# Instance norm on one core: 32 units of 4 MB become four of 4 MB and fourteen of 8 MB with 64 KB rows

## The chip, the cores and the metric

The kernel runs on one core of a Trainium2 chip. The metric is device time in microseconds (us) of one execution, as the median of several. The core has a matrix engine (PE), a vector engine (DVE), a scalar engine (ACT), a general engine (POOL), a sequencer for transfers (SP), and 16 DMA engines that move data between the device memory and the on-chip memory. SP and ACT each have a hardware DMA queue of their own (q1 is that of SP, q10 that of ACT); both queues feed the same 16 DMA engines.

## The reference

Each of 4 x 8 x 16 = 512 channels of 256 x 256 float32 is normalised by its own mean and variance, and scaled by a gamma that is shared over the batch. Input and output are 134.2 MB each.

```python
x: (4, 8, 16, 256, 256) float32, gamma: (8, 16) float32
mu = x.mean(axis=(3, 4), keepdims=True)
var = ((x - mu) ** 2).mean(axis=(3, 4), keepdims=True)
x_norm = (x - mu) / np.sqrt(var + 1e-5)
out = x_norm * gamma[None, :, :, None, None]
```

## The kernel before

The input is one flat array, cut into U = 32 units of 128 rows (one row per partition) by F = 8192 elements. A row is 32 KB, a unit is 4 MB, and a channel takes S = 8 rows, so that a unit holds K = 16 channels. A unit lives in one of AHEAD = 6 slots (`xt`) of on-chip memory.

The work of one unit, in the loop from line 104 on:

- DVE sums each row (`reduce_sum`, line 106) while ACT squares the same row and accumulates the squares (line 107; the squares themselves go to `junk`). Both results go to `st`.
- PE multiplies `st` with `navg`, a matrix that holds -1/65536 where two rows belong to the same channel (line 115). The result `ps` has minus the mean and minus the mean square of a row's channel, in every row.
- A short chain over one column follows: `nvar` on DVE (116), `std` on ACT (120), `rstd` and `scale` on DVE (124, 126).
- DVE normalises the unit in place (line 135). In unit 0 alone ACT does three eighths of it (line 132), and needs a `shift` for that (line 131).
- ACT's queue stores the unit (line 139). Then SP's queue loads the unit that is to use the same slot (lines 141 and 48), once that store has landed.

The order within each engine is the order of the program: nothing reorders it. The first six loads are issued before everything else, units 1 and 3 on ACT's queue and the others on SP's. All stores are on ACT's queue. Before the loop POOL fills `navg`, and PE spreads gamma over the rows of `g_col` from `g_rep`, a copy with each gamma repeated (lines 80 to 91). A `touch` of 16 x 128 zeros is written to the output early by POOL (lines 52 to 54): 512 bytes at the start of every eighth row of unit 0, which the store of unit 0 writes over later.

Of the kernel before, what the change touches and what calls it, by code (L numbers as in the profile page):

```python
# [1 line left out]

# [4 lines left out]

F32 = mybir.dt.float32
U8 = mybir.dt.uint8
ALU = mybir.AluOpType  # L10
ACTF = mybir.ActivationFunctionType
AX = mybir.AxisListType


@with_exitstack
def kernel(
    ctx: ExitStack,
    tc: tile.TileContext,
    x: bass.AP,
    gamma: bass.AP,  # L20
    out: bass.AP,
):
    nc = tc.nc
    B, G, C, H, W = x.shape
    P = nc.NUM_PARTITIONS
    HW = H * W
    n_ch = B * G * C
    S = 8
    K = P // S
    F = HW // S  # L30
    U = n_ch // K
    NG = (G * C) // K
    AHEAD = 6
    assert HW % S == 0 and (G * C) % K == 0

    xv = x.rearrange("b g c h w -> (b g c h w)").rearrange("(u p f) -> u p f", p=P, f=F)
    ov = out.rearrange("b g c h w -> (b g c h w)").rearrange("(u p f) -> u p f", p=P, f=F)
    gv = gamma.rearrange("g c -> (g c)")

    data = ctx.enter_context(tc.tile_pool(name="data", bufs=1))  # L40
    singles = ctx.enter_context(tc.tile_pool(name="singles", bufs=1))
    psum = ctx.enter_context(tc.tile_pool(name="psum", bufs=4, space=bass.MemoryType.PSUM))
    ctx.enter_context(tc.manual_schedule())

    slots = [data.tile([P, F], F32, name=f"xt{i}") for i in range(AHEAD)]

    def load(u, queue):
        queue.dma_start(out=slots[u % AHEAD][:], in_=xv[u])  # L48


    g_row = singles.tile([1, G * C], F32, name="g_row")
    touch = singles.tile([16, 128], F32, name="touch")
    nc.vector.memset(touch[:], 0.0)  # L53
    nc.gpsimd.dma_start(out=ov[0][0::S, 0:128], in_=touch[:])  # L54
    nc.gpsimd.dma_start(out=g_row[:], in_=gv[None, :])  # L55
    for u in range(AHEAD):
        load(u, nc.scalar if u in (1, 3) else nc.sync)

    eps_t = singles.tile([P, 1], F32, name="eps_t")
    nc.gpsimd.memset(eps_t[:], 1e-5)  # L60
    one = singles.tile([1, 1], F32, name="one")
    nc.gpsimd.memset(one[:], 1.0)
    navg = singles.tile([P, K, S], F32, name="navg")
    nc.gpsimd.memset(navg[:], -1.0 / HW)  # L64
    nc.gpsimd.affine_select(  # L65
        out=navg[:], in_=navg[:], pattern=[[-S, K], [0, S]], compare_op=ALU.is_ge,
        fill=0.0, base=0, channel_multiplier=1,
    )
    nc.gpsimd.affine_select(  # L69
        out=navg[:], in_=navg[:], pattern=[[S, K], [0, S]], compare_op=ALU.is_ge,  # L70
        fill=0.0, base=S - 1, channel_multiplier=-1,
    )
    navg_w = navg[:].rearrange("p k s -> p (k s)")
    root_eps = singles.tile([P, 1], F32, name="root_eps")
    nc.scalar.activation(out=root_eps[:], in_=eps_t[:], func=ACTF.Sqrt)  # L75
    g_rep = singles.tile([1, NG, K, S], F32, name="g_rep")
    g_ps = psum.tile([P, NG], F32, name="g_ps", bufs=1)
    g_col = singles.tile([P, NG], F32, name="g_col")

    nc.vector.tensor_copy(  # L80
        out=g_rep[:],
        in_=g_row[:].rearrange("o (n k) -> o n k", n=NG).unsqueeze(3).to_broadcast([1, NG, K, S]),
    )
    for n in range(NG):
        nc.tensor.matmul(  # L85
            out=g_ps[:, n : n + 1],
            lhsT=g_rep[:, n].rearrange("o k s -> o (k s)"),
            rhs=one[:],
            start=True, stop=True,
        )  # L90
    nc.vector.tensor_copy(out=g_col[:], in_=g_ps[:])  # L91

    junk = singles.tile([P, F], U8, name="junk")

    st = singles.tile([P, U, 2], F32, name="st")
    nvar = singles.tile([P, U], F32, name="nvar")
    std = singles.tile([P, U], F32, name="std")
    rstd = singles.tile([P, U], F32, name="rstd")
    scale = singles.tile([P, U], F32, name="scale")

    shift = singles.tile([P, 1], F32, name="shift")

    squares = []
    for u in range(U):
        t = slots[u % AHEAD]
        nc.vector.reduce_sum(out=st[:, u, 0:1], in_=t[:], axis=AX.X)  # L106
        square = nc.scalar.activation(  # L107
            out=junk[:], in_=t[:], func=ACTF.Square, accum_out=st[:, u, 1:2],
        )
        if u:  # L110

            tc.declare_no_dep(square.ins, squares[-1].ins, reason="junk, ordered by the root between")
        squares.append(square)
        ps = psum.tile([P, 2], F32, name="ps")
        nc.tensor.matmul(out=ps[:], lhsT=navg_w, rhs=st[:, u], start=True, stop=True)  # L115
        nc.vector.tensor_scalar(  # L116
            out=nvar[:, u : u + 1], in0=ps[:, 0:1], scalar1=ps[:, 0:1],
            scalar2=ps[:, 1:2], op0=ALU.mult, op1=ALU.add,
        )
        nc.scalar.activation(  # L120
            out=std[:, u : u + 1], in_=nvar[:, u : u + 1], func=ACTF.Sqrt,
            bias=eps_t[:], scale=-1.0,
        )
        nc.vector.reciprocal(out=rstd[:, u : u + 1], in_=std[:, u : u + 1])  # L124
        g = u % NG
        nc.vector.tensor_mul(  # L126
            out=scale[:, u : u + 1], in0=rstd[:, u : u + 1], in1=g_col[:, g : g + 1],
        )
        cut = F * 5 // 8 if u == 0 else F
        if cut < F:  # L130
            nc.vector.tensor_mul(out=shift[:], in0=ps[:, 0:1], in1=scale[:, u : u + 1])  # L131
            nc.scalar.activation(  # L132
                out=t[:, cut:], in_=t[:, cut:], func=ACTF.Identity, bias=shift[:], scale=scale[:, u : u + 1],
            )
        nc.vector.tensor_scalar(  # L135
            out=t[:, :cut], in0=t[:, :cut], scalar1=ps[:, 0:1], scalar2=scale[:, u : u + 1],
            op0=ALU.add, op1=ALU.mult,
        )
        nc.scalar.dma_start(out=ov[u], in_=t[:])
        if u + AHEAD < U:  # L140
            load(u + AHEAD, nc.sync)


# [1 line left out]
_INS = ['x', 'gamma']  # L145
_OUTS = [((4, 8, 16, 256, 256), 'float32')]


# [23 lines left out]
```

## Time and profile before

| What | Value |
|---|---|
| Time, median of 3 runs | 626.87 us (626.64 to 627.07) |
| Span of the profiled execution, first to last instruction | 625.2 us |
| Profiled execution outside its span, taken as median less span | 1.7 us |
| DVE busy | 441.8 us (71%) |
| ACT busy | 241.8 us (39%) |
| PE busy | 21.4 us (3%) |
| Moved by the DMA engines | 268.46 MB, mean 429 GB/s |
| Load of a unit (SP's queue), issue to landing, median | 38.5 us |
| Store of a unit (ACT's queue), issue to landing, median | 62.5 us |

The profile page gives busy times, the span in 40 slices with the share of the time in which the DMA engines were busy, the DMA queues with their share of the 16 engines' time, and the costliest groups of instructions with what they waited for. "Share of 16 engines" means that 100% would be all 16 engines busy from the first to the last instruction. The trace also has a record of each single DMA packet (queue, size, start and duration); where a packet's duration is told in the text, it is from these records. In this kernel each row of 32 KB is one packet.

### The profile page before, as it was taken

The numbers are of one execution on the slowest core, as the hardware profiler recorded it, in microseconds if no ns is written. First come the engines' busy times: TensorE is split into PE (matmuls) and PEld (weight loads), VectorE is DVE, ScalarE is ACT, GpSimd is POOL, SyncE is SP. The second block draws the span as 40 slices with busy tenths as digits, with TensorE's granted clock in tenths as the row PEclk, the third lists the DMA queues.
The fourth block names the chain that finished last, engine by engine and source line by source line (L and its number), as shares of the span: only waits on it lengthen the run. The fifth ranks groups of instructions, "written<-read, shape, count | busy, mean of one in ns | idle before, by whom it ended". The sixth has DMA issues, their size and how long they took to land.

```text
span 625.2 us, 635 instructions
## 1 busy us (share of the span) xinstructions
PE 21.4 (3%) x80; PEld 19.5 (3%) x80; DVE 441.8 (71%) x164; ACT 241.8 (39%) x99; POOL 2.4 (0%) x11
## 2 busy tenths in 40 slices
PE   0200000000000000000000000000000000000000
PEld 0200000000000000000000000000000000000000
DVE  0589999998776687666786767867668676687730
ACT  0464444444443244432344423444224442244400
POOL 1000000000000000000000000000000000000000
DMA  8999999999999999999999999999999999999998
GB/s 370 436 407 432 436 436 436 436 436 430 423 436 434 434 428 434 434 436 436 436 436 428 426 436 436 432 430 434 434 436 436 436 436 421 432 436 434 434 430 367
DMA packets 9282, 268.46 MB, mean 429 GB/s; under 512 B 1072, under 2 KB 1088, under 8 KB 1088
## 3 DMA queue, kind: packets, MB, share of 16 engines
q10 hardware_dynamic: 4896, 142.61, 52.9%
q1 hardware_dynamic: 4320, 125.83, 46.8%
q0 software_dynamic: 64, 0.01, 0.0%
q14 instruction: 2, 0.02, 0.0%
HBM read 134.22 MB, written 134.23 MB: 429 GB/s over the span
## 4 chain that ended last, share of the span: by engine, by line
another core or an unknown queue 61%; DMA 17%; DVE 15%; SPq 1%; PE 1%; issue 0%; ACT 0%
DMA xt<-in_x_dram 10%; DVE st L106 10%; DMA out_dram<-xt 8%; DVE xt L135 5%; SPq L48 1%; PE ps L115 1%; ACT std L120 0%; DVE nvar L116 0%; DVE rstd L124 0%; DVE scale L126 0%; DVE shift L131 0%
## 5 line engine op out<-in xcount | busy, mean ns | idle before, releaser
L106 DVE TENSOR_REDUCE st<-xt 128x1 f32<-128x8192 f32 x32 | 277.9, 8684 | 102.2 <-DMA xt<-in_x_dram 102.2
L107 ACT ACTIVATE junk<-xt 128x8192 uint8<-128x8192 f32 x32 | 225.0, 7030 | 272.0 <-DMA xt<-in_x_dram 233.8
L135 DVE TENSOR_SCALAR xt<-xt,ps,scale 128x8192 f32<-128x8192 f32 (+1 forms) x32 | 144.0, 4500 | 1.1
L120 ACT ACTIVATE std<-nvar,eps_t 128x1 f32<-128x1 f32 x32 | 9.4, 295 | 79.4 <-DVE nvar L116 79.4
L115 PE MATMUL ps<-st,navg 128*128 128x2 f32 x64 | 17.8, 348 | 557.3 <-DVE st L106 557.3
L115 PEld LDWEIGHTS ps<-st,navg 128*128 128x128 f32 x64 | 16.0, 310 | 559.1 <-issue 546.2
L116 DVE TENSOR_SCALAR nvar<-ps 128x1 f32<-128x1 f32 x32 | 9.2, 286 | 23.8 <-PE ps L115 23.8
L124 DVE RECIPROCAL rstd<-std 128x1 f32<-128x1 f32 x32 | 5.2, 163 | 11.6 <-ACT std L120 11.6
L80 DVE COPY g_rep<-g_row 1x1024 f32<-1x1024 f32 x1 | 0.7, 681 | 14.4 <-DMA g_row<-in_gamma_dram 14.4
L107 ACT ACTIVATION_READ_ACCUMULATOR junk<-xt 128x1 f32 x32 | 6.0, 186 | 0.0
L126 DVE TENSOR_TENSOR scale<-rstd,g_col 128x1 f32<-128x1 f32 x32 | 5.1, 158 | 1.1
L85 PE MATMUL g_ps<-one,g_rep 1*128 1x1 f32 x16 | 3.5, 347 | 16.3 <-DVE g_rep L80 16.3
L85 PEld LDWEIGHTS g_ps<-one,g_rep 1*128 1x128 f32 x16 | 3.5, 326 | 16.3 <-issue 16.3
L132 ACT ACTIVATE xt<-xt,shift,scale 128x3072 f32<-128x3072 f32 x1 | 2.9, 2947 | 0.7 <-DVE shift L131 0.7
L91 DVE COPY g_col<-g_ps 128x8 f32<-128x8 f32 x1 | 0.2, 167 | 3.7 <-PE g_ps L85 3.7
L75 ACT ACT_TABLE_LOAD x1 | 1.3, 1283 | 1.7 <-PEq L156 1.7
L53 DVE MEMSET touch<- 16x128 f32 x1 | 0.2, 165 | 0.9 <-PEq L156 0.9
L54 POOL DMA_DIRECT2D out_dram<-touch x1 | 0.6, 617 | 0.8 <-DVE touch L53 0.8
L55 POOL DMA_DIRECT2D g_row<-in_gamma_dram x1 | 0.5, 487 | 0.0
L65 POOL TENSOR_SCALAR_AFFINE_SELECT navg<-navg 128x128 f32<-128x128 f32 x1 | 0.4, 400 | 0.1
L69 POOL TENSOR_SCALAR_AFFINE_SELECT navg<-navg 128x128 f32<-128x128 f32 x1 | 0.4, 399 | 0.1
L64 POOL MEMSET navg<- 128x128 f32 x1 | 0.2, 230 | 0.0
(8 smaller groups left out, 1.0 us busy)
## 6 DMA issues: line engine op xcount, KB each, us to landing
out_dram<-xt ACTq DMA_DIRECT2D x32, 4096.0 KB, 62.5
xt<-in_x_dram SPq DMA_DIRECT2D x30, 4096.0 KB, 38.5
xt<-in_x_dram ACTq DMA_DIRECT2D x2, 4096.0 KB, 31.7
out_dram<-touch POOLq DMA_DIRECT2D x1, 8.0 KB, 9.3
g_row<-in_gamma_dram POOLq DMA_DIRECT2D x1, 0.5 KB, 13.5
```

What stands on the lines that cost most here:

```text
L48: queue.dma_start(out=slots[u % AHEAD][:], in_=xv[u])
L75: nc.scalar.activation(out=root_eps[:], in_=eps_t[:], func=ACTF.Sqrt)
L85: nc.tensor.matmul(out=g_ps[:, n : n + 1], lhsT=g_rep[:, n].rearrange("o k s -> o (k s)"), rhs=one[:], start=True, stop=True,)
L106: nc.vector.reduce_sum(out=st[:, u, 0:1], in_=t[:], axis=AX.X)
L107: square = nc.scalar.activation(out=junk[:], in_=t[:], func=ACTF.Square, accum_out=st[:, u, 1:2],)
L115: nc.tensor.matmul(out=ps[:], lhsT=navg_w, rhs=st[:, u], start=True, stop=True)
L116: nc.vector.tensor_scalar(out=nvar[:, u : u + 1], in0=ps[:, 0:1], scalar1=ps[:, 0:1], scalar2=ps[:, 1:2], op0=ALU.mult, op1=ALU.add,)
L120: nc.scalar.activation(out=std[:, u : u + 1], in_=nvar[:, u : u + 1], func=ACTF.Sqrt, bias=eps_t[:], scale=-1.0,)
L124: nc.vector.reciprocal(out=rstd[:, u : u + 1], in_=std[:, u : u + 1])
L126: nc.vector.tensor_mul(out=scale[:, u : u + 1], in0=rstd[:, u : u + 1], in1=g_col[:, g : g + 1],)
L132: nc.scalar.activation(out=t[:, cut:], in_=t[:, cut:], func=ACTF.Identity, bias=shift[:], scale=scale[:, u : u + 1],)
L135: nc.vector.tensor_scalar(out=t[:, :cut], in0=t[:, :cut], scalar1=ps[:, 0:1], scalar2=scale[:, u : u + 1], op0=ALU.add, op1=ALU.mult,)
```

## The change

The unit of work is no longer always 4 MB. `sizes` has four units of 4 MB (128 rows of 32 KB) and then fourteen of 8 MB (128 rows of 64 KB; a channel takes S = 4 rows there). The on-chip memory is the same 24 MB, now as three pairs of halves: a 4 MB unit takes half a pair, an 8 MB unit a whole one.

- Loads and stores of the 8 MB units are one DMA each with rows of 64 KB, but for `halved_loads` (units 4 and 5 are loaded as two column halves, two DMAs with rows of 32 KB each) and `halved_stores` (units 15 and 17, the last, are normalised and stored by column halves).
- An 8 MB unit is summed and squared in two halves of 8192 columns, and PE adds the two halves up (two matmuls into one `ps`). The column chain and, but for the halved ones, the normalising are done once for each unit.
- ACT helps with three eighths of the normalising in units 0, 16 and 17 (`helped`), where it helped in unit 0 only.
- A load is issued when the stores of what was in its place have been issued in the program, and it waits until they have landed: an 8 MB load waits for the whole pair.
- `touch` and its write are gone.
- There are two matrices `navg` and two spreads `g_col`, for S = 8 and S = 4.

The core of the diff:

```diff
-    AHEAD = 6
-    xv = x.rearrange("b g c h w -> (b g c h w)").rearrange("(u p f) -> u p f", p=P, f=F)
-    slots = [data.tile([P, F], F32, name=f"xt{i}") for i in range(AHEAD)]
+    F = 8192
+    HALVES = 6
+    sizes = [1] * 4 + [2] * ((n_half - 4 - 0) // 2) + [1] * 0
+    U = len(sizes)
+    starts = [sum(sizes[:i]) for i in range(U)]
+    halved_loads = (4, 5)
+    halved_stores = (U - 3, U - 1)
+    helped = (0, U - 2, U - 1)
+    def rows(flat, u):
+        lo = starts[u] * P * F
+        return flat[lo : lo + sizes[u] * P * F].rearrange("(p f) -> p f", p=P)
+    pairs = [data.tile([P, 2 * F], F32, name=f"xt{i}") for i in range(HALVES // 2)]
...
+    pending = []
+    for u in range(U):
+        if u in halved_loads and sizes[u] == 2:
+            pending += [(u, 0, F, starts[u] + 1), (u, F, 2 * F, starts[u] + 2)]
+        else:
+            pending += [(u, 0, sizes[u] * F, starts[u] + sizes[u])]
+    def load(stored):
+        while pending and pending[0][3] <= stored + HALVES:
+            u, lo, hi, _ = pending.pop(0)
+            t, c = home(u)
+            queue = nc.scalar if u in (1, 3) else nc.sync
+            queue.dma_start(out=t[:, c + lo : c + hi], in_=rows(xf, u)[:, lo:hi])
...
-    touch = singles.tile([16, 128], F32, name="touch")
-    nc.vector.memset(touch[:], 0.0)
-    nc.gpsimd.dma_start(out=ov[0][0::S, 0:128], in_=touch[:])
...
+        for h in range(sizes[u]):
+            part = t[:, c + h * F : c + (h + 1) * F]
+            at = starts[u] + h
+            nc.vector.reduce_sum(out=st[:, at, 0:1], in_=part, axis=AX.X)
+            square = nc.scalar.activation(
+                out=junk[:], in_=part, func=ACTF.Square, accum_out=st[:, at, 1:2],
+            )
...
+        for h in range(sizes[u]):
+            nc.tensor.matmul(
+                out=ps[:], lhsT=navg[S], rhs=st[:, starts[u] + h],
+                start=h == 0, stop=h == sizes[u] - 1,
+            )
...
+        step = F if u in halved_stores else cols
+        for lo in range(0, cols, step):
+            mid, hi = lo + step, lo + step
+            if u in helped:
+                mid = lo + step * 5 // 8
+                nc.scalar.activation(
+                    out=t[:, c + mid : c + hi], in_=t[:, c + mid : c + hi], func=ACTF.Identity,
+                    bias=shift[:, u : u + 1], scale=scale[:, u : u + 1],
+                )
+            nc.vector.tensor_scalar(
+                out=t[:, c + lo : c + mid], in0=t[:, c + lo : c + mid], scalar1=ps[:, 0:1],
+                scalar2=scale[:, u : u + 1], op0=ALU.add, op1=ALU.mult,
+            )
+            nc.scalar.dma_start(out=rows(of, u)[:, lo:hi], in_=t[:, c + lo : c + hi])
+        load(starts[u] + sizes[u])
```

More of the change, by code (lines that the diff above doesn't have):

```diff
@@ L43, with home @@
     ctx.enter_context(tc.manual_schedule())
-    slots = [data.tile([P, F], F32, name=f"xt{i}") for i in range(AHEAD)]
-    def load(u, queue):
-        queue.dma_start(out=slots[u % AHEAD][:], in_=xv[u])
+    pairs = [data.tile([P, 2 * F], F32, name=f"xt{i}") for i in range(HALVES // 2)]
+    def home(u):
+        at = starts[u] % HALVES
+        return pairs[at // 2], (at % 2) * F
+    pending = []
[10 more added lines that the diff above has]
+            queue.dma_start(out=t[:, c + lo : c + hi], in_=rows(xf, u)[:, lo:hi])
     g_row = singles.tile([1, G * C], F32, name="g_row")
-    touch = singles.tile([16, 128], F32, name="touch")
-    nc.vector.memset(touch[:], 0.0)
-    nc.gpsimd.dma_start(out=ov[0][0::S, 0:128], in_=touch[:])
     nc.gpsimd.dma_start(out=g_row[:], in_=gv[None, :])
-    for u in range(AHEAD):
-        load(u, nc.scalar if u in (1, 3) else nc.sync)
+    load(0)
     eps_t = singles.tile([P, 1], F32, name="eps_t")
@@ L62 @@
     nc.gpsimd.memset(one[:], 1.0)
[L63 to L73, printed above, removed]
+    navg, g_col = {}, {}
@@ new lines @@
+    for S in (8, 4):
+        K = P // S
+        w = singles.tile([P, K, S], F32, name=f"navg{S}")
+        nc.gpsimd.memset(w[:], -1.0 / HW)
+        nc.gpsimd.affine_select(
+            out=w[:], in_=w[:], pattern=[[-S, K], [0, S]], compare_op=ALU.is_ge,
+            fill=0.0, base=0, channel_multiplier=1,
+        )
+        nc.gpsimd.affine_select(
+            out=w[:], in_=w[:], pattern=[[S, K], [0, S]], compare_op=ALU.is_ge,
+            fill=0.0, base=S - 1, channel_multiplier=-1,
+        )
+        navg[S] = w[:].rearrange("p k s -> p (k s)")
@@ L74 @@
     root_eps = singles.tile([P, 1], F32, name="root_eps")
     nc.scalar.activation(out=root_eps[:], in_=eps_t[:], func=ACTF.Sqrt)
[L76 to L89, printed above, removed]
-        )
@@ L91 @@
-    nc.vector.tensor_copy(out=g_col[:], in_=g_ps[:])
+    g_all = singles.tile([1, G * C * 8], F32, name="g_all")
+    for S in (8, 4):
+        K = P // S
+        n_g = (G * C) // K
+        g_rep = g_all[:, : G * C * S].rearrange("o (c s) -> o c s", s=S)
+        nc.vector.tensor_copy(
+            out=g_rep, in_=g_row[:].unsqueeze(2).to_broadcast([1, G * C, S]),
+        )
+        g_ps = psum.tile([P, n_g], F32, name=f"g_ps{S}", bufs=1)
+        g_col[S] = singles.tile([P, n_g], F32, name=f"g_col{S}")
+        for n in range(n_g):
+            nc.tensor.matmul(
+                out=g_ps[:, n : n + 1],
+                lhsT=g_all[:, n * P : (n + 1) * P],
+                rhs=one[:],
+                start=True, stop=True,
+            )
+        nc.vector.tensor_copy(out=g_col[S][:], in_=g_ps[:])
@@ L99 @@
     scale = singles.tile([P, U], F32, name="scale")
-    shift = singles.tile([P, 1], F32, name="shift")
+    shift = singles.tile([P, U], F32, name="shift")
     squares = []
     for u in range(U):
[L105 to L113, printed above, removed]
-        ps = psum.tile([P, 2], F32, name="ps")
-        nc.tensor.matmul(out=ps[:], lhsT=navg_w, rhs=st[:, u], start=True, stop=True)
+        t, c = home(u)
+        S = 8 // sizes[u]
+        cols = sizes[u] * F
+        for h in range(sizes[u]):
[5 more added lines that the diff above has]
+            )
+            if squares and h == 0:
+                tc.declare_no_dep(square.ins, squares[-1].ins, reason="junk, ordered by the root between")
+            squares.append(square)
+        ps = psum.tile([P, 2], F32, name="ps")
+        for h in range(sizes[u]):
+            nc.tensor.matmul(
+                out=ps[:], lhsT=navg[S], rhs=st[:, starts[u] + h],
+                start=h == 0, stop=h == sizes[u] - 1,
+            )
         nc.vector.tensor_scalar(
@@ L124 @@
         nc.vector.reciprocal(out=rstd[:, u : u + 1], in_=std[:, u : u + 1])
-        g = u % NG
+        g = (starts[u] * (P // 8) % (G * C)) // (P // S)
         nc.vector.tensor_mul(
-            out=scale[:, u : u + 1], in0=rstd[:, u : u + 1], in1=g_col[:, g : g + 1],
+            out=scale[:, u : u + 1], in0=rstd[:, u : u + 1], in1=g_col[S][:, g : g + 1],
         )
[L129 to L133, printed above, removed]
-            )
[L135 to L141, printed above, removed]
+        if u in helped:
+            nc.vector.tensor_mul(out=shift[:, u : u + 1], in0=ps[:, 0:1], in1=scale[:, u : u + 1])
+        step = F if u in halved_stores else cols
+        for lo in range(0, cols, step):
+            mid, hi = lo + step, lo + step
+            if u in helped:
+                mid = lo + step * 5 // 8
+                nc.scalar.activation(
+                    out=t[:, c + mid : c + hi], in_=t[:, c + mid : c + hi], func=ACTF.Identity,
+                    bias=shift[:, u : u + 1], scale=scale[:, u : u + 1],
+                )
+            nc.vector.tensor_scalar(
+                out=t[:, c + lo : c + mid], in0=t[:, c + lo : c + mid], scalar1=ps[:, 0:1],
+                scalar2=scale[:, u : u + 1], op0=ALU.add, op1=ALU.mult,
+            )
+            nc.scalar.dma_start(out=rows(of, u)[:, lo:hi], in_=t[:, c + lo : c + hi])
+        load(starts[u] + sizes[u])
+    assert not pending
 _INS = ['x', 'gamma']
```

15 lines of the change are left out of this document (6 added, 9 removed).

## The prediction, made before the changed kernel ran

> **What bounds the kernel now.** I read the page's slices and DMA queues first, then the sync engine's own waits, then narrow windows at the end, and last the timeline of the last unit.
>
> ```profile
> DMA  8999999999999999999999999999999999999998
> q10 hardware_dynamic: 4896, 142.61, 52.9%
> q1 hardware_dynamic: 4320, 125.83, 46.8%
> ```
>
> The two queues together fill 52.9 + 46.8 = 99.7% of the 16 DMA engines' time over the whole span. No engine of compute comes near: DVE is busy 71%, and it idles because loads are not there yet. The waits of the queue SP say the same from the other side:
>
> ```profile
> SPq L48 <- DMA out_dram<-xt: 514.7, 26, 39.7
> ```
>
> 26 loads sat ready to be issued, 514.7 us in all, until a store had landed in their slot. So only three things can shorten the run: less DMA time for the same bytes, less time before the first packet, or less after the last. The windows give the price of a row:
>
> ```profile
> core 0: us, PE busy (x) PEld busy (x) DVE busy (x) ACT busy (x) POOL busy (x), PEclk, DMA share, GB/s
> 602.00:603.00 1.00, 0.00 (x0) 0.00 (x0) 0.00 (x0) 0.00 (x0) 0.00 (x0) 1.00 1.21 524
> 623.00:624.00 1.00, 0.00 (x0) 0.00 (x0) 0.00 (x0) 0.00 (x0) 0.00 (x0) 1.00 0.01 0
> ```
>
> 524 GB/s in 1 us is 16 rows of 32,768 bytes counted where they start, one for each engine, and a share of 1.21 says that each took 1.21 us. The packet records have 1,213 ns for nearly all rows and 1,209.5 ns from start to start. A completion packet of 4 bytes closes each DMA on each engine (9 ns; it delays the next row by 9.5 ns). Each engine carries 512 rows and 64 completions. Span: first row at 1.8, 512 x 1.2095 = 619.3, 64 x 0.0095 = 0.6, from the last row (623.9) to the end 1.3; that leaves 625.2 - 623.0 = 2.2 us of stalls. Of these the records place some 0.6 us in the first rows (they took 1.83 us in the mean), about 0.8 near 40 us, where the first store's rows and the loads beside them took 1.3 to 2.0 us, and a few tenths in single gaps of about 0.5 us. The median of the runs is 1.7 us above this span; I carry that unchanged.
>
> ```profile
> 585.57 8.69 DVE L106 TENSOR_REDUCE st<-xt 128x1 f32<-128x8192 f32 x1 [4.33 <-DMA xt<-in_x_dram]
> ...
> 596.03 4.55 DVE L135 TENSOR_SCALAR xt<-xt,ps,scale 128x8192 f32<-128x8192 f32 x1
> ```
>
> In the last unit the sum takes 8.69 us, the chain to the normalising 1.8 (594.26 to 596.03), the normalising 4.55, and the store is issued at 600.62, 15.0 us after its load landed. The stores still queued at 585.6 cover that: DMA stays busy to 623.9.
>
> **Rows of 64 KB.** The count of DMAs goes from 64 to 40: loads 4 + 4 (halves) + 12, stores 4 + 4 (halves) + 12. On each engine 24 x 8 = 192 rows of 64 KB take the place of 384 of 32 KB, and 128 rows of 32 KB stay. The gain is the fixed part f of a row, once for each of 192. No row of the trace has 64 KB, so I bound f by packets of other sizes: 4 bytes take 9 ns, which is nearly all fixed; the line through 512 bytes (27 ns) and 32 KB (1,213) leaves 8.2; that through 8 KB (307, instruction fetches) and 32 KB leaves 5.0. If a row costs by the byte alone, f is 0. So the gain lies between 0 and 192 x 9 = 1.7 us. I take 7 ns, between the two lines, since both rest on real data packets: 192 x 7 = 1.35 us. The 24 completions fewer give 24 x 9.5 = 0.23 us.
>
> The Trainium skill has a ceiling for these transfers (DMA: Bandwidth & Descriptors, "Where 436 GB/s comes from": 16 ports x 32 bytes x 850 MHz, 435.2 GB/s). By that an estimate of f is 1,209.5 - 1,204.7 = 4.8 ns, and the gain would be 0.9 in place of 1.35 us. The trace's 433.5 GB/s between row starts agrees with a ceiling just above it.
>
> **The missing touch.** Its 16 packets cost 27 ns each, nothing. Whether it makes the first store's rows quicker the trace can't say: with it they took 0.25 us more than others in the mean. The nearest row for a first access with nothing ahead of it is the first load's, 0.6 us over. So the cost is 0 to 0.6, perhaps a little below; I take 0.15, as the larger part of the stall near 40 us is in load rows, which the touch doesn't write.
>
> **The start.** Same loads on the same two queues, so the first row is due at 1.8 and unit 0 at 22.8. More set-up stands ahead on DVE: a second copy of gamma, 4 more columns on PE (16 matmuls took 3.54, so 8 take 1.8) and a copy out, about 2.6 us after the 20.06 at which `g_col` was done: 22.7, just before the first load lands. Hidden, and if it came later, six loads (6 x 9.7 = 58 us of rows) cover it. POOL's three added instructions (1.0 us) end before 6 us. The two queued halves of unit 5 wait for stores 0 and 1 as loads 6 and 7 did.
>
> **The middle.** For an 8 MB unit the DMA work is 2 x 8 x 2.42 = 38.7 us; DVE needs 2 x 8.69 + 1.8 + 2 x 4.55 = 28.3, ACT two squares of 7.2 and little else. Three pairs now stand where six slots did: one in compute, one loading, one storing. Call a load's landing 0. The store of the unit ahead was issued at 28.3 - 38.7 = -10.4, shares the engines row by row, and lands near +31; the next load is issued on that, while the load before it still has 6 us of rows left. Both queues keep work, and cost is nothing as long as that cover lasts. A missing 6 us would begin to cost only after the store queue too had run dry. A store on ACT waits for the normalising; behind it in ACT's order are the next unit's squares, which are done within DVE's time.
>
> **The end.** Here there is no refill, so I followed the rows of the last three units. Call 0 the end of load 16's rows. It lands at 1.5 (unit 0's landing came about that long after its last row). Load 17 was issued near -5, when store 14 landed. Unit 15's halves were issued near -12 and -8, so that about 18 us of its 19.4 are left at 0. Load 17 has 8 rows of 2.42 us on each engine, and I let the engine alternate row by row, so that 8 rows of 1.21 go with them: load 17 ends at 29, lands at 30.5. Left for the store queue at 29: 8.3 of unit 15 and all 19.3 of unit 16 (issued at 1.5 + 17.4 + 1.8 + 5.9 = 26.6, with ACT's help), so it runs dry near 57. The first half of store 17 is issued at 30.5 + 17.4 + 1.8 + 2.95 = 52.6. Its first row comes 1.0 us later (first load: 0.8 to 1.8) to 3.4 later (first store: 36.5 to 39.9), 53.6 to 56.0. Cover left: 1 to 3.4 us. The second half follows 3.3 us behind, well inside 9.7 us of rows. Without help in unit 16 or the halves of 17 this would be a gap; with them I count nothing.
>
> **Sum.** -1.35 - 0.23 + 0.15 = -1.43 us, span 623.8, time 625.4.
>
> **Rivals.**
> A row of 64 KB goes out as two packets (chance 0.12). No trace row is that long. Then f stays, and at the end load 17 alternates 32 KB against 32 KB: its 16 rows go with all that is left of unit 15, it ends at 38 and lands at 39.5, store 17 is issued at 61.6 and has rows at 62.6 to 65.0, while the queue ran dry at 38 + 19.7 = 57.7. The gap is 5 to 7 us, say 6: 626.87 - 0.23 + 0.15 + 6 = 632.8, slower. It decides once load 17 lands more than the cover of 1 to 3.4 us late. Against it: in the trace a row is one packet, whatever the DMA.
> A row's time is by bytes alone (0.12): 626.87 - 0.23 + 0.15 = 626.8, no change.
> Rows at twice the pitch are slower (0.06). 28 of 32 halves change pitch, 543 us of rows, so that each percent costs 5.4 us: 630.9 for one percent. The trace has rows of one pitch alone, which run within 0.3% of each other, for loads and stores alike. The Trainium skill warns of pitches at large powers of two (DMA: Bandwidth & Descriptors, "Latency and other measured facts": 512 KiB already loses 3%, 2 MiB more); 64 KB lies far below its smallest entry, and no run here shows it.
>
> **How the numbers follow.** The forecast has 0.70, with f of 0 to 9 ns and the touch giving 624.8 to 626.9, mostly 624.9 to 626.0. A measurement of this kernel tells some 0.2% (1.25 us) from no change, so faster means below 625.6, which the forecast meets about three times in four: 0.52. Same is the rest of it and the second rival: 0.28. Slower is the first and the third with a little for a cover of 1 us used up: 0.20. The range 624.5 to 628.2 leaves out the split and the pitch.
>
> **What would show it.** Right: 192 long rows an engine, at 2.415 to 2.42 us; DMA queues at 99.7% of a span near 623.8; 40 DMAs; no dark slice; store 17's first half issued about 22 us after the last landing, with no gap in the windows there. Wrong: packets of 32 KB only and an empty stretch of several us some 20 us before the end; or long rows above 2.426 us; or a longer stall near 40 us, where the first store begins without the touch.

## The result: slower by 0.6%

The changed kernel takes 630.89 us (median of four runs, 628.72 to 631.58); the kernel before took 626.76 beside it (626.64 to 627.07). The ratio is 1.0059, with a 95% interval of 1.0041 to 1.0076. That is 4.1 us slower, where 1.4 us faster was forecast, and outside the range. The profiled execution took 630.39 us.

These lines of its page answer to those shown of the kernel before:

```profile
span 628.7 us, 554 instructions
...
DMA  8999999999999999999999999999999999999997
...
q10 hardware_dynamic: 3168, 142.61, 52.5%
q1 hardware_dynamic: 2592, 125.83, 46.9%
```

At first sight nothing has changed: no dark slice, and the two queues fill 99.4% of the span. But the shares have to be multiplied by the span. Before, 99.7% of 625.2 is 623.3 us of work for each DMA engine; now 99.4% of 628.7 is 624.9. The same bytes kept each engine busy 1.6 us longer, although there were fewer rows and completions. Beside that, 3.8 us of the span are idle, where 1.9 were. A DMA share counts a row as busy for as long as it takes, so a row that crawls looks like a row that works.

SP's queue still sits waiting for stores as before, 518.8 us in all, in 14 waits where there were 26:

```profile
SPq L75 <- DMA out_dram<-xt: 518.8, 14, 39.5
```

The packet records place the time. I took the time of each row over the median of its size, summed it and divided by 16 engines; I call this **slow rows** below. It was 1.6 us before and is 5.0 us now, of which 3.3 are 64 KB rows of loads and 0.4 are 64 KB rows of stores. The account is this: the engines' last rows end at 625.8 in the mean, where it was 623.3, that is +2.5 = -1.1 (fewer rows and completions) + 3.4 (slow rows) + 0.2 (small gaps). The last engine ends 1.6 us behind that mean where it was 0.6, another +1.0; most of this is a fetch of 16 KB of instructions, for which one engine left its rows for 0.93 us from 601.84 on. In the kernel before, that fetch came at 625.63, behind the last row. Together the end of the data moves by 3.4 us, and the span by 3.5.

The worst place is the first 64 KB load, from 125 us on. Windows of the changed kernel show it (share is the time of the rows that start in the window, GB/s their bytes):

```profile
core 0: us, PE busy (x) PEld busy (x) DVE busy (x) ACT busy (x) POOL busy (x), PEclk, DMA share, GB/s
122.00:125.00 3.00, 0.00 (x0) 0.00 (x0) 3.00 (x1) 3.00 (x1) 0.00 (x0) 1.00 1.17 459
125.00:128.00 3.00, 0.00 (x0) 0.00 (x0) 3.00 (x1) 2.42 (x2) 0.00 (x0) 1.00 1.00 306
128.00:131.00 3.00, 0.56 (x2) 0.50 (x2) 1.82 (x5) 0.29 (x1) 0.00 (x0) 1.00 0.66 262
131.00:134.00 3.00, 0.00 (x0) 0.00 (x0) 3.00 (x1) 0.00 (x0) 0.00 (x0) 1.00 0.97 415
```

The same stretch of the kernel before:

```profile
119.00:131.00 12.00, 0.55 (x2) 0.50 (x2) 10.83 (x6) 5.06 (x2) 0.00 (x0) 1.00 1.01 437
```

Bytes over share is the rate of the rows themselves. Before it is 437 / 1.01 = 433 GB/s. In the window from 125 us it is 306 / 1.00: those rows took 1.4 times as long as rows at full rate. The records have single rows of up to 4.33 us there, where the median is 2.418. Some 1.4 us of the loss lie in this place; the rest is scattered over nearly every later load, mostly in rows that begin 5 to 13 us after a store began. These are also the first rows of the load itself, up to 8 us behind its first one.

### The profile page after: what moved, and what is told of

It reads as the page before. It is cut to its first block, busy times and chain, and to the rows that moved or that the text cites. A ratio compares the mean times of both kernels' runs of the same rounds, so it can differ in the third digit from the quotient of the medians.

```text
span 628.7 us, 554 instructions
## 1 busy us (share of the span) xinstructions
PE 23.3 (4%) x88; PEld 21.3 (3%) x88; DVE 422.8 (67%) x113; ACT 249.1 (40%) x88; POOL 3.1 (0%) x13
## 4 chain that ended last, share of the span: by engine, by line
DMA 59%; DVE 28%; another core or an unknown queue 6%; ACT 1%; PE 1%; issue 0%; SPq 0%; ACTq 0%
DMA xt<-in_x_dram 30%; DMA out_dram<-xt 29%; DVE st L140 19%; DVE xt L177 8%; ACT xt L173 1%; PE ps L149 1%; ACT std L157 0%; DVE nvar L153 0%; DVE rstd L161 0%; DVE scale L163 0%; SPq L75 0%; ACTq L181 0%; DVE shift L167 0%
## 5 line engine op out<-in xcount | busy, mean ns | idle before, releaser
L177 DVE TENSOR_SCALAR xt<-xt,ps,scale 128x16384 f32<-128x16384 f32 (+3 forms) x20 | 134.0, 6709 | 0.6
L157 ACT ACTIVATE std<-nvar,eps_t 128x1 f32<-128x1 f32 x18 | 5.3, 295 | 63.8 <-DVE nvar L153 63.8
L173 ACT ACTIVATE xt<-xt,shift,scale 128x3072 f32<-128x3072 f32 (+1 forms) x4 | 14.3, 3587 | 2.4 <-DVE shift L167 2.0
L153 DVE TENSOR_SCALAR nvar<-ps 128x1 f32<-128x1 f32 x18 | 5.2, 287 | 13.4 <-PE ps L149 13.4
L161 DVE RECIPROCAL rstd<-std 128x1 f32<-128x1 f32 x18 | 2.9, 163 | 6.5 <-ACT std L157 6.5
L114 PE MATMUL g_ps<-one,g_all 1*128 1x1 f32 x24 | 5.4, 347 | 12.0 <-DVE g_all L108 12.0
L114 PEld LDWEIGHTS g_ps<-one,g_all 1*128 1x128 f32 x24 | 5.3, 324 | 12.0 <-issue 11.4
L163 DVE TENSOR_TENSOR scale<-rstd,g_col 128x1 f32<-128x1 f32 x18 | 2.9, 159 | 0.6
```

The costliest lines, as they stand in the source:

```text
L114: nc.tensor.matmul(out=g_ps[:, n : n + 1], lhsT=g_all[:, n * P : (n + 1) * P], rhs=one[:], start=True, stop=True,)
L153: nc.vector.tensor_scalar(out=nvar[:, u : u + 1], in0=ps[:, 0:1], scalar1=ps[:, 0:1], scalar2=ps[:, 1:2], op0=ALU.mult, op1=ALU.add,)
L157: nc.scalar.activation(out=std[:, u : u + 1], in_=nvar[:, u : u + 1], func=ACTF.Sqrt, bias=eps_t[:], scale=-1.0,)
L163: nc.vector.tensor_mul(out=scale[:, u : u + 1], in0=rstd[:, u : u + 1], in1=g_col[S][:, g : g + 1],)
L173: nc.scalar.activation(out=t[:, c + mid : c + hi], in_=t[:, c + mid : c + hi], func=ACTF.Identity, bias=shift[:, u : u + 1], scale=scale[: ...
L177: nc.vector.tensor_scalar(out=t[:, c + lo : c + mid], in0=t[:, c + lo : c + mid], scalar1=ps[:, 0:1], scalar2=scale[:, u : u + 1], op0=ALU ...
```

## The experiments

### Does the pitch or the length of the rows cost it?

The first three runs change nothing but the two lists of units whose transfers are cut into column halves. Cut, a row is 32 KB long and still lies at a pitch of 64 KB.

```diff
# e1_halves_all
-    halved_loads = (4, 5)
-    halved_stores = (U - 3, U - 1)
+    halved_loads = tuple(range(4, U))
+    halved_stores = tuple(range(4, U))
# e2_halved_stores
-    halved_stores = (U - 3, U - 1)
+    halved_stores = tuple(range(4, U))
# e3_halved_loads
-    halved_loads = (4, 5)
+    halved_loads = tuple(range(4, U - 2))
```

> The changed kernel, with every 8 MB unit loaded and stored by column halves: all rows are 32 KB, their starts stay 64 KB apart. Three theories for the 3.3 us per engine that 64 KB load rows lost beyond their usual 2.418 us (page after: scattered, mostly in the first two rows of each load). Pitch theory (reads 64 KB apart, in step on 16 engines, collide in memory): the loss stays with short rows, time 629 us or more. Dry queue theory (a load that begins after a stretch with stores alone pays in its first rows): loads now wait for halves, the load queue is always filled, time as the kernel before, 626.4 to 627.0. Row length theory (a 64 KB row is itself the trouble): also 626.4 to 627.0.

> The changed kernel, with all 8 MB units stored by halves (32 KB rows) and loads in 64 KB rows as they were. Alternating row by row, a load then gets two thirds of the engines, ends early, and the load queue lies dry for some 10 us in each unit, longer than in the changed kernel. Dry queue theory: at least the loss of the changed kernel, 630 to 632. Row length theory with the loads as the cause: 629 to 631. Row length theory with the mix of two long rows as the cause: 627. Pitch theory: 629 to 631.

> The changed kernel, with the loads of units 4 to 15 by halves (32 KB rows, 64 KB apart) and stores in 64 KB rows; both halves of a load still wait for a whole store. Row length theory with the loads as the cause: no loss, 626 to 627. Dry queue theory: the load queue is still refilled once a unit, 629 to 631. Pitch theory: 629 to 631. If the last loads are slowed by stores with long rows, a gap before the last store adds to each.

| Kernel | Loads, stores of the 8 MB units | Time, us | Ratio to before (95%) |
|---|---|---|---|
| e1_halves_all | 32 KB, 32 KB | 627.67 | 1.0009 (1.0001 to 1.0018) |
| e2_halved_stores | 64 KB, 32 KB | 628.85 | 1.0031 (1.002 to 1.0042) |
| after | 64 KB, 64 KB | 630.89 | 1.0059 (1.0041 to 1.0076) |
| e3_halved_loads | 32 KB, 64 KB | 666.37 | 1.0617 (1.0586 to 1.0648) |

The page of e1 with everything cut:

```profile
span 626.0 us, 620 instructions
...
q10 hardware_dynamic: 4896, 142.61, 52.8%
q1 hardware_dynamic: 4320, 125.83, 46.7%
```

99.5% of 626.0 is 622.9 us of work, as little as before. Slow rows are 1.5 us, and hardly any lies behind the first 60 us. So units of 8 MB, three pairs, the pitch and the later compute cost 0.8 us together, and transfers in rows of 64 KB the other 3.3. The rows of e1 have the same pitch as those of the changed kernel, so the pitch can't be what costs those 3.3; e5 below, with the pitch alone, loses nothing. The Trainium skill's warning of row pitches (DMA: Bandwidth & Descriptors, "Latency and other measured facts") begins at 512 KiB; in e5 a pitch of 64 KB shows no loss.

e2 lies between, but the profiled execution of it was the fastest of its runs, and its 64 KB load rows lost 0.35 us only. The profile thus doesn't show what the other runs of e2 lost.

e3 is the surprise: with only the loads cut back, it is 39 us slower.

```profile
span 670.0 us, 580 instructions
...
GB/s 376 438 407 438 438 438 432 391 344 344 368 352 428 444 399 430 427 432 411 401 403 413 421 436 360 381 432 434 407 432 428 409 436 383 380 436 381 380 187 346
...
q10 hardware_dynamic: 3168, 142.61, 51.8%
q1 hardware_dynamic: 4032, 125.83, 44.9%
```

Two things add up. The engines are busy 96.7% of 670.0 = 647.9 us, 24.6 more than before, and the slow rows are 27.0 us: 16.6 in the 64 KB rows of stores, 9.3 in loads. In the slices from 117 to 200 us the rate falls to 344 GB/s with no idle time. And 22.1 us are idle (187 GB/s near the end). A queue's turn is one row whatever its length: in e8 below, which has the same two lengths, 112 load rows of 32 KB begin within the 128 rows of 64 KB of the first store, one between each two on each engine. By the times of these rows (1.21 and 2.42 us) 32 KB loads get an estimated third of the engines; loads then arrive late, and the store queue runs dry.

### Is it the transfers, or how slots come back?

e4 keeps the kernel before with its 32 KB rows, and lets slots come back 8 MB at a time. The next four runs compute nothing: three 8 MB pairs are loaded on SP's queue and stored on ACT's, with rows cut or whole.

```diff
# e4_pairs, on the kernel before, units 0 to 23
+        elif u % 2:
+            for v in (u - 1, u):
+                nc.scalar.dma_start(out=ov[v], in_=slots[v % AHEAD][:])
+            for v in (u, u - 1):
+                load(v + AHEAD, nc.sync)
```

```python
# the copies: cuts() gives two halves or the whole
    def load(u):
        for lo, hi in cuts(LOAD_HALVES):
            nc.sync.dma_start(out=pairs[u % 3][:, lo:hi], in_=xv[u][:, lo:hi])
    for u in range(3):
        load(u)
    for u in range(U):
        for lo, hi in cuts(STORE_HALVES):
            nc.scalar.dma_start(out=ov[u][:, lo:hi], in_=pairs[u % 3][:, lo:hi])
        if u + 3 < U:
            load(u + 3)
```

> The kernel before (32 KB rows, 32 KB apart), but for units 0 to 23 two stores are issued together and the next two loads wait for both: slots are given back by 8 MB, as in the changed kernel. If giving slots back by 8 MB is what costs (dry queue theory, whatever the rows): 629 to 631. Pitch theory and row length theory: no change, 626.5 to 627.2.

> All computation is left out: x is copied to the output through three pairs of 8 MB, loads on SP's queue and stores on ACT's, both by column halves (32 KB rows, 64 KB apart). A store waits for its load, a load for the stores of its pair. Both theories: the floor of short rows, some 619 us of rows, 0.6 of completions, 2 to 3 of start and stalls, 1.3 at the end and 1.7 outside the span: 624 to 628.

> The copy, with loads and stores as whole 8 MB units (64 KB rows). Row theory (long store rows beside load rows are slow in themselves): slower than the copy with short rows by 3 us or more, with load or store rows of more than 2.418 us throughout. Schedule theory (slots given back by 8 MB and the waits around the compute are to blame): faster than the copy with short rows by about 1 us.

> The copy, loads in 64 KB rows, stores in 32 KB rows. Row theory with the stores as the cause: within 1 us of the copy with short rows. Row theory with the loads as the cause: slower by 3 us or more. Schedule theory: within 1 us.

> The copy, loads in 32 KB rows, stores in 64 KB rows, without the starved compute that halved loads had in the kernel. Row theory with the stores as the cause: slowest of the four, store rows of 2.6 us and more, slower than the copy with short rows by 10 us or more (in the kernel with halved loads store rows lost 16.6 us on each engine). Schedule theory: within 1 us of the copy with short rows.

| Kernel | Time, us | Ratio to before (95%) | Slow rows, us |
|---|---|---|---|
| e4_pairs | 627.42 | 1.0006 (0.9997 to 1.0014) | 1.4 |
| e5, loads 32 KB, stores 32 KB | 627.02 | 1.0000 (0.9991 to 1.001) | 1.7 |
| e6, 64 KB, 64 KB | 632.39 | 1.009 (1.0065 to 1.0115) | 5.1 |
| e7, 64 KB, 32 KB | 627.66 | 1.0015 (1.0006 to 1.0025) | 3.1 |
| e8, 32 KB, 64 KB | 654.40 | 1.0422 (1.0394 to 1.0451) | 25.7 |

Slots that come back by 8 MB are not the cause. A copy with short rows takes what the kernel before takes: its compute is hidden already, and its floor is that of the transfers. Without any compute the long rows crawl as in the changed kernel: 5.1 us of slow rows in e6 against 1.7 in e5, nearly the 5.0 against 1.6 of after and before.

The times of e6 must be read with care, though. The windows of the last 25 us, e6 first, then e5:

```profile
600.00:612.00 12.00, 0.00 (x0) 1.00 0.60 257
612.00:624.00 12.00, 0.00 (x0) 1.00 1.01 437
```

```profile
600.00:612.00 12.00, 0.00 (x0) 1.00 1.00 431
612.00:624.00 12.00, 0.00 (x0) 1.00 0.91 393
```

In e6 the last store waits for the whole last load, while the other queue has run dry: 12 x 0.40 = 4.8 us are lost there. The profiled execution of e6 has a span 7.9 us longer than that of e5. The larger part is this gap, which the changed kernel does not have; the slow rows are 3.4 us more, and fewer rows and completions take a little off. Only the slow rows carry over.

In e8 such a gap takes some 7 us, but most is slow rows again:

```profile
span 655.7 us, 123 instructions
...
q10 hardware_dynamic: 2304, 134.22, 49.4%
q1 hardware_dynamic: 4608, 134.22, 49.2%
```

98.6% of 655.7 is 646.5 us of work; e5 has 99.7% of 625.1 = 623.2 for the same bytes. So the 23 us belong to rows, with no compute in the kernel at all.

### Queue, proportion, or length?

```diff
# e9_copy_l32_s64_swapped, on e8: loads on ACT's queue, stores on SP's
-            nc.sync.dma_start(out=pairs[u % 3][:, lo:hi], in_=xv[u][:, lo:hi])
+            nc.scalar.dma_start(out=pairs[u % 3][:, lo:hi], in_=xv[u][:, lo:hi])
-            nc.scalar.dma_start(out=ov[u][:, lo:hi], in_=pairs[u % 3][:, lo:hi])
+            nc.sync.dma_start(out=ov[u][:, lo:hi], in_=pairs[u % 3][:, lo:hi])
# e10_copy_l16_s32: half the size of everything, six slots of 4 MB
-    F = 8192
-    STORE_HALVES = True
+    F = 4096
+    STORE_HALVES = False
# e11_copy_l32_s48_16, on e5: stores of 48 KB and 16 KB rows
-        for lo, hi in cuts(STORE_HALVES):
+        for lo, hi in [(0, 3 * F // 2), (3 * F // 2, 2 * F)]:
# e12_before_no_touch, the kernel before without lines 52 to 54
-    touch = singles.tile([16, 128], F32, name="touch")
-    nc.vector.memset(touch[:], 0.0)
-    nc.gpsimd.dma_start(out=ov[0][0::S, 0:128], in_=touch[:])
```

> The copy with 32 KB load rows and 64 KB store rows (654.4 us), with the queues exchanged: loads on ACT's, stores on SP's. Direction theory (long rows that go to device memory): 650 us or more again. Queue theory (long rows on ACT's queue, or the queue that is served second): 626 to 630.

> The copy in 4 MB units and six slots, loads by halves (16 KB rows), stores whole (32 KB rows): the store row is again twice the load row, but not over 32 KB. Ratio theory (store rows longer than load rows are what costs): 645 us or more. Length theory (store rows over 32 KB are): 627 to 632, with 16 rows more for each 4 MB load, at a few ns of fixed cost each.

> The copy with 32 KB load rows, each 8 MB unit stored by two DMAs of 48 KB and 16 KB rows. If store rows over 32 KB cost in proportion to their excess, about half of the 27 us of the 64 KB rows in the same place: 636 to 644. If only 64 KB rows cost: 626 to 630. If every row over 32 KB costs its full price: 645 or more.

> The kernel before without the touch of the output (lines 52 to 54). The prediction gave its removal 0 to 0.6 us, 0.15 as the value. If the touch does nothing: within 0.2 us of the kernel before, first store rows at 1.21 us in the records. If it warms the path to the output: slower by 0.3 us or more, first store rows longer.

| Kernel | Time, us | Ratio to before (95%) |
|---|---|---|
| e9, 32 KB, 64 KB, queues exchanged | 655.09 | 1.0453 (1.0437 to 1.0469) |
| e10, 16 KB, 32 KB | 643.24 | 1.0259 (1.0245 to 1.0273) |
| e11, 32 KB, 48 and 16 KB | 626.69 | 0.9995 (0.9986 to 1.0004) |
| e12, before without touch | 626.94 | 0.9999 (0.999 to 1.0008) |

e9 shows that it goes by direction and not by queue: stores twice as long as loads cost the same on either. e10 shows that no row over 32 KB is needed for it. None of its rows is longer than those of the kernel before, yet slow rows take 14.0 us, with 2.6 us of gap at the end; a theory by length alone gives no such loss. In e11, stores of 48 KB cost nothing: 6 of their 2,048 rows took over 1% longer than the median. But each is followed by a store of 16 KB rows, so that its stores and loads have the same number of rows.

The proportion is not enough either. In the records of e9 no row of 64 KB takes over 2.418 us from 40 to 160 us, and from 320 to 560 the slow rows are 13.1 us, with rows of the same two lengths throughout. Its windows (the last two numbers are DMA share and GB/s) show the full rate first and less later:

```profile
40.00:160.00 120.00, 0.00 (x0) 1.00 1.00 433
...
320.00:440.00 120.00, 0.00 (x0) 1.00 1.00 409
```

In e8 it is alike (0.0 us from 40 to 80, 12.1 from 320 to 560). Something builds up in the course of such a run; what it is was not found. The touch is worth nothing.

### Is it the dry queue?

With three slots a queue has nothing for a while between two transfers, and the engines give the other queue two rows running. The records show it, if each row is matched to the row that ended where it starts (they do not name the engine): from 130 to 560 us the kernel before changes queue at every one of 5,682 steps from row to row, while the changed one stays on its queue at some 390 of 2,875. The next runs bring this about with 32 KB rows (three and four contiguous slots of 4 MB), try 48 KB in both directions, and try to make the dry spell longer by an ACT operation ahead of each store.

```diff
# e13_copy_l32_s32_3slots, e14_copy_l32_s32_4slots: the copy with 4 MB units, whole
+    F = 4096
+    LOAD_HALVES = False
+    STORE_HALVES = False
# three slots in e13; in e14 each 3 of the slots becomes 4
# e15_copy_l48_s48_4slots: 21 units of 6 MB and one of 2 MB
+    W = 3 * F // 2
+    SLOTS = 4
# e16_copy_3slots_late_3us, on e13 (e17_copy_3slots_late_6us: 6144 columns)
+        nc.scalar.activation(out=junk[:], in_=pairs[u % 3][:, :3072], func=ACTF.Square)
```

> The copy with 32 KB rows, contiguous, in 4 MB units and only three slots: each queue is refilled by one unit at a time, as with 64 KB rows in three slots of 8 MB, at half the size. Length theory (rows over 32 KB lose when both directions have them): no loss, 626 to 628. Refill theory (with three slots both queues run dry once a unit, the 16 engines restart at different row ends, fall out of step, and reads then run beside writes): the loss of the 64 KB copy comes back with short rows, 631 us or more, and in the records the 16 engines are no longer all loading or all storing together.

> The same with four slots of 4 MB. Length theory: 626 to 628. Refill theory: less than with three slots, as one of the two queues then holds a unit more: 626 to 630, engines in step most of the time.

> The copy with 48 KB rows in both directions, contiguous, 21 units of 6 MB in four slots and a last one of 2 MB. Length theory: a loss between that of 32 KB (none) and 64 KB (5.5 us), 628 to 631. Refill theory: as with four slots of short rows, and a little faster if that one has no loss: 625.5 to 628.

> The copy with 32 KB rows and three slots of 4 MB (627.1 us), where ACT does a square of 3072 columns (some 2.95 us) between a load's landing and its store, so that the store queue lies dry for longer, near 5 us in place of 2.4, as in the 64 KB copy (4.8 us). Dry time theory (a dry spell of more than some 4 us costs at the restart, whatever the rows): 630 us or more. Length theory (64 KB rows in both directions cost by themselves): 626.5 to 627.5.

> The same with a square of 6144 columns (some 5.9 us): the store queue lies dry for about 8 us each time. Dry time theory: 632 us or more. Length theory: 626.5 to 628, with the engines of the DMA still never idle.

| Kernel | Time, us | Ratio to before (95%) |
|---|---|---|
| e13, 32 KB, three slots | 627.12 | 1.0001 (0.9991 to 1.0011) |
| e14, 32 KB, four slots | 627.01 | 1.0001 (0.9992 to 1.001) |
| e15, 48 KB, four slots | 626.68 | 0.9997 (0.9987 to 1.0006) |
| e16, e13 with a late store | 627.14 | 1.0012 (0.9996 to 1.0028) |
| e17, later still | 627.04 | 1.0000 (0.999 to 1.0009) |

In e13 each queue is dry for two rows, 2.4 us, at every unit, so that some 715 of 5,682 steps stay on their queue, much the same share as in the changed kernel, and nothing is lost: dry queues alone do not do it. Nor do engines that have fallen out of step. From 130 to 560 us 4.8 of the 16 engines in e13 run in the rarer direction in the mean, 5.2 in the changed kernel and 2.8 in the kernel before. A loss that grows evenly with the length of the rows falls too, because 48 KB in both directions costs nothing:

```profile
span 624.9 us, 124 instructions
...
q1 hardware_dynamic: 3168, 134.22, 50.0%
q10 hardware_dynamic: 3168, 134.22, 49.6%
```

The added ACT work of e16 and e17 did not do its task: the dry spell stayed at 2.4 us. So these two say nothing on whether 4.8 us, which the changed kernel has, would hurt rows of 32 KB.

### Stores of 48 KB in the changed kernel

```diff
# e18_stores_48_16, on the changed kernel
-            nc.scalar.dma_start(out=rows(of, u)[:, lo:hi], in_=t[:, c + lo : c + hi])
+            cut = lo + step * 3 // 4 if step == 2 * F else hi
+            for a, b in ((lo, cut), (cut, hi)):
+                if a < b:
+                    nc.scalar.dma_start(out=rows(of, u)[:, a:b], in_=t[:, c + a : c + b])
```

> The changed kernel, loads in 64 KB rows as they were, with the whole stores of 8 MB units cut into two DMAs of 48 KB and 16 KB rows (units 15 and 17 stay in halves); computation and waits for the slots are the same. If 64 KB store rows beside 64 KB load rows are what costs: the loss is gone, 626 to 627.5. If 64 KB load rows or the return of slots by 8 MB cost: 629 to 631.

It takes 629.05 us, a ratio of 1.003 (1.0018 to 1.0041): about half of the loss is gone, as in e2. Its profile, taken of its fastest run:

```profile
span 626.4 us, 581 instructions
...
q10 hardware_dynamic: 4896, 142.61, 52.9%
q1 hardware_dynamic: 2592, 125.83, 46.7%
```

99.6% of 626.4 is 623.9 us of work, 1.0 less than in the changed kernel. The 64 KB rows of the loads lost 1.1 us: 0.9 near 125 us, where the changed kernel has its worst place too, and 0.2 in all later units, where the changed kernel lost 2.2. In these profiles, then, the load rows behind the first long load run undisturbed once the stores beside them are shorter. They do so although the dry spells are longer than in the changed kernel: the load queue is dry for some 12 us in each unit of e2 and 10 in e18, the store queue for 4.8 in both. As these are the fastest executions of both, this is a sign and no proof.

No version beat the kernel before: e5, e11 and e15, which compute nothing, are at its time.

## Why the prediction was wrong

**The step that failed** is in "The middle", where it says "Both queues keep work, and cost is nothing as long as that cover lasts", together with the count of rows in "Rows of 64 KB". Every long row was priced at one fixed duration, whatever runs beside it. The median did come out as forecast (2.418 us; "2.415 to 2.42"), but the mean of the load rows was 2.452, and 193 of 1,536 took over 1% longer than the median. These rows hold 3.3 of the 5.0 us of slow rows; the sum had none, and slow rows grew by 3.4. The prediction had named the sign ("long rows above 2.426 us"), and its only rival with slower rows was the pitch. That rival's 630.9 is close to the time by luck, as its cause is not the one: e1 and e5 have the pitch without the loss. In the kernel before, all rows were of one length, which is why nothing in its trace spoke of it.

**The cover in the middle** failed too. "6 us of rows left" when the next load is issued was worked out with the delays of short rows. In the trace most loads are issued with 2.0 us left (236.65, where the load ahead ends at 238.68), and their first row comes 4.2 us later. So each queue is dry for 4.8 us once in a unit, two rows of the other queue, where the kernel before has one between any two rows. A completion now waits for a 64 KB row of the other queue: the last row of unit 7's load ends at 199.82 by the records, and the sum begins 2.8 us later, where in the last unit before it was 1.6.

```profile
202.60 8.69 DVE L140 TENSOR_REDUCE st<-xt 128x1 f32<-128x8192 f32 x1 [8.35 <-DMA xt<-in_x_dram]
```

That dry queues cost by themselves is not shown: e13 has them and loses nothing.

**The fixed part of a row** exists, and was a little too large. A 64 KB row is one packet, against the first rival. From start to start it takes 2,414.3 ns where two of 32 KB take 2,419.0, so the fixed part is 4.7 ns where 7 was taken. With 24 completions fewer that is 1.1 us in place of 1.6. The estimate of 4.8 ns from the ceiling of the Trainium skill ("Where 436 GB/s comes from", in DMA: Bandwidth & Descriptors) agrees with the 4.7.

**The touch** was priced at 0.15 us; e12 shows nothing. The reading of "the first store's rows" near 40 us was wrong: the first store's rows begin at 43.25, behind a load in the same queue, and take 1.213 us. The stall there is in load rows, with or without the touch. The 3.4 us from issue to first row that the end uses ("first store: 36.5 to 39.9") rest on the same reading; no run shows them.

**The start** was right as to cost: the first row comes at 1.81 and unit 0 lands at 22.7. `g_col` was ready at 17.6 already, where 22.7 was forecast.

**The end** came as worked out, within some 1 us at each step but one:

```profile
575.95 0.34 ACTq L181 DMA_DIRECT2D out_dram<-xt  x1
...
580.85 17.28 DVE L140 TENSOR_REDUCE st<-xt 128x1 f32<-128x8192 f32 x2 [5.01 <-DMA xt<-in_x_dram]
...
599.99 5.80 DVE L177 TENSOR_SCALAR xt<-xt,ps,scale 128x5120 f32<-128x5120 f32 x2
...
603.09 0.34 ACTq L181 DMA_DIRECT2D out_dram<-xt  x1
```

The first line is the store of unit 16, the second the landing of load 17, the last the first half of store 17, issued 22.2 us after that landing (forecast 22.1). Counted from the end of load 16's rows (549.45), load 17 was issued at -2.0 (forecast -5), landed at 31.4 (30.5), and the first half of store 17 was issued at 53.6 (52.6). The rows of unit 16 end between 605.37 and 608.00 on the 16 engines, and those of store 17 follow at once, the first at 605.37, 2.3 us after the issue. So the cover held; rows of one queue come in order, and the records can't say how much of it was left. The windows show no gap there, only the rows that are thinning out at the very end:

```profile
604.00:606.00 2.00, 0.00 (x0) 0.00 (x0) 1.79 (x1) 2.00 (x1) 0.00 (x0) 1.00 0.91 393
...
624.00:626.00 2.00, 0.00 (x0) 0.00 (x0) 0.00 (x0) 0.00 (x0) 0.00 (x0) 1.00 0.50 213
626.00:628.00 2.00, 0.00 (x0) 0.00 (x0) 0.00 (x0) 0.00 (x0) 0.00 (x0) 1.00 0.04 16
```

The unequal end of the engines, +1.0 us, was not in the sum.

**What stays open.** Why 64 KB in both directions, or stores twice as long as loads, slow the rows was not found, nor why the second loss grows in the course of a run. In the changed kernel the rows that crawl begin shortly after a store starts on the other queue. Length and the dry time that comes with it (4.8 against 2.4 us) were not told apart in runs where both directions have long rows, as e16 and e17 missed; the profiles of e2 and e18 speak against the dry time alone. Nor was it settled why the medians of e2 and e18 keep some 2 us over the kernel before, while their profiled executions, each the fastest of its runs, show 0.3 and 1.2 us more span.

## What to carry to other kernels

Where transfers alone bound a kernel, first write a copy of the same size without compute: here it took 627.0 us, as long as the kernel before, and said that its compute cost nothing; what was left to win by longer rows was a microsecond of fixed parts. Larger transfers are no gain by themselves. In the runs here rows of the same length in both directions were free at 32 and 48 KB, and stores with rows twice as long as those of the loads were the dearest; so try lengths on a copy and keep to one that it shows to be free. A share of 99% says only that the engines were occupied; multiply it by the span and compare the work with the bytes.

## What was not expected of the hardware

- Rows of 16, 32, 48 and 64 KB take 611, 1,213, 1,815 and 2,418 ns undisturbed, a straight line. Disturbed, a 64 KB row took up to 4.33 us, and a 32 KB row 2.8 us.
- An engine takes one row from each queue in turn (5,682 of 5,682 steps before), whatever the length (112 short rows within 128 long ones in e8's first store). So row length sets the share of the engines that a queue gets. The Trainium skill tells of turns of whole packets of some 9 to 17 descriptors (DMA: Bandwidth & Descriptors, "Queues, rings and completion order"); with these rows the records show turns of one row.
- Stores with rows twice as long as those of the loads cost 27 us in a copy at 64 and 32 KB (e8) and 16 us at 32 and 16 KB (e10), the gaps at the end included; in e9 the same rows ran undisturbed from 40 to 160 us. Loads twice as long as stores cost 0.6 us (e7).
